# Attention projections in pairs of blocks: seven products of quarters for eight, score work in units of two tiles, smaller buffers

## The chip, the cores and the metric

The kernel runs on one core of one Trainium2 chip. The metric is device time in microseconds, the median of several executions. Engines: TensorE (PE), VectorE (DVE), ScalarE (ACT), GpSimd (POOL), SyncE (SP).

## The reference

One encoder layer on 1024 tokens of 1024 channels. The part that matters is the attention branch; the recurrent branch, the gates, the merge and a mixture of 16 experts follow it.

```python
h = _rmsnorm(x, norm_g)
proj = jnp.einsum('bsd,de->bse', h, w_in) + b_in
parts = jnp.split(proj, _split_points(), axis=-1)
...
for g, (window, dilation) in enumerate(ATTN_GROUPS):    # (128, 1), (512, 4), (2048, 16)
    shp = (B, S, HEADS_PER_GROUP, HEAD_DIM)             # 4 heads of 128
    q = _partial_rotary(q_parts[g].reshape(shp), cos, sin)
    k = _partial_rotary(k_parts[g].reshape(shp), cos, sin)
    v = v_parts[g].reshape(shp)
    o, lse = _dilated_window_attention(q, k, v, window // (2 * dilation), dilation)
    outs.append(o)
    lses.append(lse)
wts = jax.nn.softmax(jnp.stack(lses, axis=0), axis=0)
o = jnp.sum(wts[..., None] * jnp.stack(outs, axis=0), axis=0)
```

So for each of 4 heads and 3 groups there are three projections (q, k, v) of 1024 tokens from 1024 to 128 channels, 36 blocks of 128 channels in all.

## The kernel before

Stages follow one another: norm of x and its transposition, attention, recurrent branch and gates, merge and router, experts. Products are in float32 accuracy from reduced parts: each operand is split into a high and a low part (`split`: a cast on ACT for the high part, a subtraction on VectorE for the low), and `mm3` issues three matmuls (lines 51 to 53: high by high, high by low, low by high).

`norm_in` leaves the normed, transposed tokens in `hh` and `hl`, for each half h of the tokens [128, 8, 512]: 8 slices k of 128 channels by 512 tokens. `proj` loads no weights itself; it splits a [128, 8, 128] block `raw` into `wh`, `wl` and issues, for 2 halves by 8 slices, `mm3` into a PSUM tile `pj` of two banks: 48 matmuls of 128x512. The pool `pp` of `pj` has two such tiles and is opened ahead of `norm_in`.

`attn_head` runs a head's three groups and then combines them. `attn_group` makes q, k and v (`proj`, eviction with bias on ACT, line 260, or 243 and 245 for v with dilation under 16, which is laid out in slots of 64 keys; for q and k a rotation of the first 32 channels by a shuffle, two multiplications with the table `rot`, which stays in SBUF, and an addition, lines 264 to 268, on VectorE), transposes v (`pt`, then `vt`), and works through 8 tiles of 128 queries: scores into `ps` on TensorE, mask and row maximum on VectorE into `sc` and `stat` (line 293), minus the maxima (`nb`, line 295), exponentials with row sums on ACT, transposes into `pt`, copies to `pT` on VectorE (line 307), the products with `vt` into `po` (line 317), and copies into `og` on ACT (lines 320, 323). `og` is a ring of four buffers.

After the third group `stat` is transposed and copied to `stT` (line 333), stored to HBM and read back as `cs` in another layout; some small operations of ACT, VectorE and GpSimd (`wk`) turn it into three rows of weights, stored as `wg`. GpSimd then loads each row over all partitions into `wb` (one buffer), multiplies `og` by it, and sums into `ya`, which is stored (lines 365 to 371).

A scheduler at compile time sets the order in which each engine's instructions stand; each engine runs its own in that order. It mixes a group's TensorE work with the projections of the next blocks.

## Time and profile before

| what | us |
|---|---|
| median of 3 executions (2335.36 to 2339.7) | 2335.42 |
| the profiled execution's own time | 2332.01 |
| its span, first to last instruction | 2330.3 |
| TensorE busy in it | 2259.1 (97%) |
| VectorE busy | 1718.2 (74%) |
| ACT busy | 1391.7 (60%) |
| GpSimd busy | 217.4 (9%) |

The attention stage ends at about 537 us, the experts fill the second half. The rows for single stretches stand in the section of rows below; a row names the line of the kernel, the engine, the operation, and the tiles it writes and reads (out<-in).

### The profile page before, as it was taken

To read this page: it belongs to the slowest core of one execution; us is meant where nothing else is said; L and a number is where in the kernel's file an instruction comes from. 1 tells how busy PE (TensorE), PEld (TensorE's weight loads), DVE (VectorE), ACT (ScalarE), POOL (GpSimd) and SP (SyncE) were. 2 spreads that over 40 slices of the span, in tenths; PEclk is the share of its full clock that TensorE was granted. 3 is DMA by queue.
4 is the path that set the end of the run, shared out by engine and by line. 5 is a ranking of instruction groups with operands and counts; after the bars stand their busy time and mean duration, and the time that the engine had idled before them with its cause. 6 is when DMAs were issued, how large, how long until landed. Compare 5 with 4: busy or idle time off the path is not lost. (4 is left out here: it accounts for less than half of the span.)

```text
span 2330.3 us, 29850 instructions
## 1 busy us (share of the span) xinstructions
PE 2259.1 (97%) x10586; PEld 1852.4 (79%) x10586; DVE 1718.2 (74%) x2582; ACT 1391.7 (60%) x1725; POOL 217.4 (9%) x236
## 2 busy tenths in 40 slices
PE   7999999999999999999959999999999999999996
PEld 6887888887888888778847888888888888888884
DVE  7545454453455565678679999999999999999998
ACT  5332323324655666432137888888788888888886
POOL 1022030404000000100010000000000000000001
PEclk9999999999999999999979999999999999999999
DMA  4112121212322224745859999999999999999993
GB/s 151 37 37 80 31 82 37 74 37 87 104 77 81 69 68 150 240 159 168 320 190 338 381 380 378 377 389 389 388 379 380 380 377 389 395 385 380 378 388 127
DMA packets 238846, 539.20 MB, mean 231 GB/s; under 512 B 17628, under 2 KB 116376, under 8 KB 238696
## 3 DMA queue, kind: packets, MB, share of 16 engines
q1 hardware_dynamic: 224192, 488.70, 56.7%
q0 software_dynamic: 14400, 48.55, 6.3%
q8 instruction: 83, 1.36, 0.2%
q14 instruction: 67, 0.55, 0.1%
q10 hardware_dynamic: 104, 0.04, 0.0%
HBM read 501.35 MB, written 35.86 MB: 231 GB/s over the span
## 5 line engine op out<-in xcount | busy, mean ns | idle before, releaser
L46 DVE TENSOR_TENSOR elo<-et,ehi 128x1024 fp32r<-128x1024 f32 x549 | 648.2, 1223 | 76.3 <-ACT ehi L44 60.6
L44 ACT CAST ehi<-et 128x1024 fp32r<-128x1024 f32 x549 | 568.3, 1050 | 133.8 <-PE pg L53 89.4
L51 PE MATMUL pj<-hh,wh 128*128 128x512 f32 x1088 | 429.8, 395 | 2.1 <-ACT xp L389 2.0
L52 PE MATMUL pj<-hl,wh 128*128 128x512 f32 x1088 | 427.6, 393 | 0.0
L53 PE MATMUL pj<-hh,wl 128*128 128x512 f32 x1088 | 427.5, 393 | 0.0
L52 PE MATMUL pg<-elo,xgh 128*128 128x512 f32 x1032 | 407.6, 395 | 1.4 <-DVE elo L46 1.2
L51 PE MATMUL pg<-ehi,xgh 128*128 128x512 f32 x1032 | 403.6, 393 | 0.0
L53 PE MATMUL pg<-ehi,xgl 128*128 128x512 f32 x1032 | 402.8, 390 | 0.0
L44 ACT CAST wh<-raw 128x1024 fp32r<-128x1024 f32 (+1 forms) x100 | 98.2, 982 | 440.1 <-PE pj L52 267.8
L46 DVE TENSOR_TENSOR wl<-raw,wh 128x1024 fp32r<-128x1024 f32 x99 | 115.6, 1168 | 195.7 <-PE pj L53 191.1
L51 PEld LDWEIGHTS pj<-hh,wh 128*128 128x128 f32 x1088 | 204.7, 188 | 43.8 <-ACT xp L389 2.4
L53 PEld LDWEIGHTS pj<-hh,wl 128*128 128x128 f32 x1088 | 204.5, 188 | 41.2
L52 PEld LDWEIGHTS pj<-hl,wh 128*128 128x128 f32 x1088 | 204.8, 188 | 40.7
L52 PEld LDWEIGHTS pg<-elo,xgh 128*128 128x128 f32 x1032 | 194.2, 188 | 42.2 <-DVE elo L46 3.4
L51 PEld LDWEIGHTS pg<-ehi,xgh 128*128 128x128 f32 x1032 | 194.3, 188 | 41.1 <-ACT xgh L44 0.3
L53 PEld LDWEIGHTS pg<-ehi,xgl 128*128 128x128 f32 x1032 | 194.3, 188 | 39.4 <-DVE xgl L46 0.2
L52 PE MATMUL po<-elo,hdh 128*128 128x512 f32 x488 | 191.6, 393 | 4.0 <-DVE elo L46 4.0
L51 PE MATMUL po<-ehi,hdh 128*128 128x512 f32 x488 | 191.1, 392 | 1.7 <-ACT ehi L44 1.0
L53 PE MATMUL po<-ehi,hdl 128*128 128x512 f32 x488 | 190.0, 389 | 0.6 <-DVE hdl L46 0.6
L44 ACT CAST ehi<-raw 128x1024 fp32r<-128x1024 f32 x96 | 100.6, 1051 | 30.4 <-PE pg L53 21.7
L46 DVE TENSOR_TENSOR elo<-raw,ehi 128x1024 fp32r<-128x1024 f32 x96 | 114.5, 1221 | 3.3
L52 PEld LDWEIGHTS po<-elo,hdh 128*128 128x128 f32 x488 | 91.6, 188 | 25.5 <-DVE elo L46 6.1
(314 smaller groups left out, 3113.8 us busy)
## 6 DMA issues: line engine op xcount, KB each, us to landing
...
et<-w_down SPq DMA_DIRECT2D x177, 512.0 KB, 6.8
...
```

Of the source, the lines that this page charges most:

```text
L44: a = self.nc.scalar.copy(hi, src).ins
L46: b = (engine or self.nc.vector).tensor_sub(lo, src, f32(hi)).ins
L51: mm(ps, ah, bh, start=first, stop=False)
L52: mm(ps, ah, bl, start=False, stop=False)
L53: mm(ps, al, bh, start=False, stop=last)
```

## The change

The first two blocks (q and k of head 0, group 0) keep plain products (`one`), now in halves of 512 tokens. The other 34 are taken in pairs in the order of head, group, and q, k, v. For a pair with weights a and b, split by input channels into a1, a2 and b1, b2, and tokens split into quarters (`hq[c, h]`, 512 channels c by 512 tokens h), `pair` computes seven products of a 512x128 weight block by a quarter, 12 matmuls each, in place of eight. The combinations of the quarters, t1 to t4, are made once (`sums`), and those of the weights in each pair; two products are added to earlier ones in PSUM (`more`), the rest on VectorE when the result is put into place (`put`). t4 takes the place of the quarter b01, which is stored to HBM and loaded again behind the attention stage. Groups are called from `attention`, so that a group follows the pair that holds its v.

Beside this: PSUM tiles `pj` of one bank, four of them, in a pool opened behind `norm_in`; rotations in halves with `rot` loaded for each half, already in the group's order of tokens; scores, exponentials, transposes and products in units of two tiles (four for dilation 16), with `sc` and `pT` in two small buffers, `pT` copied on ACT, one `po` buffer; `og` in a ring of three, with the combined result formed in place in the first; `wb` in halves in one buffer, the small combination on 32 partitions.

```diff
-        self.hh = [self.hp.tile([128, 8, 512], FR, name=f"hh{h}") for h in range(2)]
-        self.hl = [self.hp.tile([128, 8, 512], FR, name=f"hl{h}") for h in range(2)]
+        self.hq = {(c, h): self.quarter(c, h) for h in range(2) for c in range(2)}
...
+    def weights(self, src, engine=None):
+
+        self.nw = (self.nw + 1) % 5
+        w = self.wp.tile([128, 2, 4, 128], FR, **({"name": "wh"} if self.nw < 3 else {"name": "wl", "bufs": 2}))
+        self.split(w[:, 0], w[:, 1], src, engine)
+        return w[:, 0], w[:, 1]
+
+    def times(self, ps, w, q, first, last, more=False):
+        for k in range(4):
+            self.mm3(ps, w[0][:, k], w[1][:, k], q[0][:, k], q[1][:, k], first and k == 0, last and k == 3, more)
+
+    def one(self, raw, out):
+
+        engine = self.nc.gpsimd if len(self.first_raws) == 2 else None
+        w = [self.weights(raw[:, 4 * c:4 * c + 4], engine) for c in range(2)]
+        for h in range(2):
+            ps = self.pp.tile([128, 512], F, name="pj")
+            for c in range(2):
+                self.times(ps, w[c], self.hq[c, h], c == 0, c == 1)
+            out(h, ps)
+
+    def sums(self, ap):
+
+        nc, hq = self.nc, self.hq
+        for part, q in enumerate(hq[0, 1]):
+            nc.sync.dma_start(self.s["b01"][part], f32(q).rearrange("p k t -> p (k t)"))
+        self.tq = [[self.tp.tile([128, 4, 512], FR, name=f"t{n}{part}") for part in "hl"] for n in range(3)]
+        rest = []
+        for c, name in enumerate(("vt", "qkv2")):
+            cs = slice(2 * c, 2 * c + 2)
+            t1, t2, t3 = [ap.tile([128, 2, 512], F, name="og", bufs=3) for _ in range(3)]
+            t4 = ap.tile([128, 2, 512], F, name=name)
+
+            def whole(t, *q):
+                hi, lo = [f32(a[:, cs]) for a in hq[q]]
+                nc.vector.tensor_add(t, hi, lo)
+
+            def parts(n, t):
+                self.split(self.tq[n][0][:, cs], self.tq[n][1][:, cs], t)
+
+            whole(t3, 0, 1)
+            whole(t1, 0, 0)
+            nc.vector.tensor_sub(t1, t3, t1)
+            whole(t2, 1, 1)
+            nc.vector.tensor_sub(t3, t2, t3)
+            nc.vector.tensor_sub(t2, t2, t1)
+            parts(1, t2)
+            parts(0, t1)
+            parts(2, t3)
+            whole(t4, 1, 0)
+            nc.vector.tensor_sub(t4, t4, t2)
+            rest.append((cs, t4))
+        q = self.quarter(0, 1)
+        for cs, t in rest:
+            self.split(q[0][:, cs], q[1][:, cs], t)
+        self.tq.append(q)
+
+    def pair(self, ap, a, b, outs):
+
+        nc, hq, (t1, t2, t3, t4) = self.nc, self.hq, self.tq
+        a1, a2, b1, b2 = a[:, :4], a[:, 4:], b[:, :4], b[:, 4:]
+        s = self.rp.tile([128, 2, 4, 128], F, name="raw128")
+        s1, s2 = s[:, 0], s[:, 1]
+        nc.vector.tensor_add(s1, b1, b2)
+        nc.vector.tensor_sub(s2, s1, a1)
+        p = lambda: self.pp.tile([128, 512], F, name="pj")
+        u, v = [ap.tile([128, 512], F, name="u" + n) for n in "12"]
+        pa = p()
+        self.times(pa, self.weights(a1), hq[0, 0], True, True)
+        nc.scalar.copy(u, pa)
+        pb = p()
+        self.times(pb, self.weights(s2), t2, True, True)
+        nc.vector.tensor_add(v, pb, u)
+        pc = p()
+        self.times(pc, self.weights(s1), t1, True, True)
+        nc.vector.tensor_sub(b1, a1, b1)
+        self.times(pb, self.weights(b1), t3, False, True, True)
+        nc.vector.tensor_add(u, pb, u)
+        outs[1](1, pc, u)
+        pd = p()
+        self.times(pd, self.weights(b2), t4, True, True)
+        outs[1](0, pd, u)
+        nc.vector.tensor_sub(s2, a2, s2)
+        self.times(pa, self.weights(a2), hq[1, 0], False, True, True)
+        outs[0](0, pa)
+        self.times(pc, self.weights(s2), hq[1, 1], False, True, True)
+        outs[0](1, pc, v)
+
...
+        n = S // d // 2
+        bias = self.b_in(j)
+        view = lambda a: a.rearrange("p (r l) -> p r l", r=d)
+
+        def out(half, ps, more=None):
+            if slots:
+                mid, end = view(t[:, :2 * d * (n - 64)]), view(t[:, 2 * d * (n - 64):])
+                to = [[(end[:, :, 64:], 0, 64), (mid[:, :, :n - 64], 64, n)],
+                      [(mid[:, :, n - 64:], 0, n - 64), (end[:, :, :64], n - 64, n)]][half]
+            else:
+                to = [(view(t)[:, :, half * n:half * n + n], 0, n)]
+            for o, a, b in to:
+                src = self.perm(ps, d)[:, :, a:b]
+                if more is None:
+                    nc.scalar.activation(o, src, AF.Identity, bias=bias)
+                else:
+                    nc.vector.scalar_tensor_tensor(o, src, bias, self.perm(more, d)[:, :, a:b], op0=OP.add, op1=OP.add)
+
+        return out
+
+    def rotate(self, ap, t, g):
+        nc = self.nc
+        for c in range(2):
+            cs = slice(c * 512, (c + 1) * 512)
+            rot = ap.tile([32, 2, 512], F, name="rot")
+            nc.sync.dma_start(rot, self.i["rot"][g, :, :, cs].rearrange("a p s -> p a s"))
+            sw = ap.tile([32, 512], F, name="sw")
+            x = t[0:32, cs]
+            nc.vector.stream_shuffle(sw, x, [(p + 16) % 32 for p in range(32)])
+            nc.vector.tensor_mul(sw, sw, rot[:, 1])
+            nc.vector.tensor_mul(x, x, rot[:, 0])
+            nc.vector.tensor_add(x, x, sw)
+
+    def attn_group(self, h, g, ap, stat, q, k, vT):
...
         tiles = self.tiles[g]
+        o = ap.tile([128, S], F, name="og", bufs=3)
...
+            sc = ap.tile([128, n, 512 // n], F, name="sc", bufs=2)
...
-            nc.vector.tensor_copy(pT[:, c:c + 4], p)
-
-        o = ap.tile([128, S], F, name="og", bufs=4)
...
+            nc.scalar.copy(pT, p)
+            if t0 % 4 == 0:
+                po = self.p3.tile([128, 4, 128], F, name="po")
...
-    def attn_head(self, h, ap):
+    def attention(self, ap):
+
+        blocks = [(h, g, w) for h in range(4) for g in range(3) for w in range(3)]
+        got = {}
+        og = []
+
+        def place(h, g, w):
+            t = got[h, g, w] = ap.tile([128, S], F, name=f"qkv{w}", bufs=2 if w == 0 else 1)
+            return self.put(t, DILS[g], 16 + 12 * w + 4 * g + h, w == 2 and DILS[g] < 16)
+
+        def finished(h, g, w):
+            if w < 2:
+                self.rotate(ap, got[h, g, w], g)
+                return
+            if g == 0:
+                self.stat = ap.tile([128, 3, 2, 8], F, name="stat", bufs=2)
+            og.append(self.attn_group(h, g, ap, self.stat, *[got.pop((h, g, i)) for i in range(3)]))
+            if g == 2:
+                self.combine(h, ap, self.stat, og)
+                og.clear()
+                if h == 0:
+                    self.decays(ap)
+
+        def load(b):
+            return self.first_raws.pop(0) if self.first_raws else self.load_w(*self.attn_cols(*b))
+
+        for b in blocks[:2]:
+            self.one(load(b), place(*b))
+        self.sums(ap)
+        for b in blocks[:2]:
+            finished(*b)
+        for n in range(2, len(blocks), 2):
+            two = blocks[n:n + 2]
+            raws = [load(b) for b in two]
+            self.pair(ap, *raws, [place(*b) for b in two])
+            for b in two:
+                finished(*b)
+
+    def combine(self, h, ap, stat, og):
         nc, s = self.nc, self.s
-        stat = ap.tile([128, 3, 2, 8], F, name="stat", bufs=2)
-        og = [self.attn_group(h, g, ap, stat) for g in range(3)]
...
-        y = ap.tile([128, S], F, name="ya", bufs=1)
+        nc.gpsimd.dma_start(s["wg"][h].rearrange("g (c i) -> c g i", c=C), wk[:, 0:3])
+        y = og[0]
         for g in range(3):
-            wb = ap.tile([128, S], F, name="wb", bufs=1)
-            src = s["wg"][h, g]
-            nc.gpsimd.dma_start(wb, bass.AP(tensor=src.tensor, offset=src.offset, ap=[[0, 128], [1, S]]))
-            if g == 0:
-                nc.gpsimd.tensor_mul(y, og[0], wb)
-            else:
-                nc.gpsimd.tensor_mul(wb, og[g], wb)
-                nc.gpsimd.tensor_add(y, y, wb)
+            for c in range(2):
+                half = slice(c * 512, (c + 1) * 512)
+                wb = ap.tile([128, 512], F, name="wb")
+                src = s["wg"][h, g, half]
+                nc.gpsimd.dma_start(wb, bass.AP(tensor=src.tensor, offset=src.offset, ap=[[0, 128], [1, 512]]))
+                nc.gpsimd.tensor_mul(og[g][:, half], og[g][:, half], wb)
+            if g:
+                nc.gpsimd.tensor_add(y, y, og[g])
         nc.gpsimd.dma_start(s["ya"][h], y)
 
 
@@ -451,21 +579,24 @@
...
-        self.pp = hs.enter_context(tc.tile_pool(name="pp", bufs=2, space=PSUM))
-        self.hp = hs.enter_context(tc.tile_pool(name="hp", bufs=1))
-        self.gp = self.hp
+        self.hp = hs.enter_context(self.pool("hp", 1))
+        self.nw = 4
         self.norm_in()
         with ExitStack() as c2:
             e2 = c2.enter_context
+            self.tp = e2(self.pool("tp", 1))
             ap = e2(self.pool("ap", 1))
+            self.pp = e2(self.pool("pp", 4, PSUM))
             self.p1 = e2(self.pool("p1", 1, PSUM))
             self.p2 = e2(self.pool("p2", 2, PSUM))
             self.p3 = e2(self.pool("p3", 1, PSUM))
...
-                self.attn_head(h, ap)
-                if h == 0:
-                    self.decays(ap)
+            self.attention(ap)
+        q = self.hq[0, 1] = self.quarter(0, 1)
+        for part in range(2):
+            nc.sync.dma_start(f32(q[part]).rearrange("p k t -> p (k t)"), self.s["b01"][part])
+        self.gp = hs.enter_context(self.pool("sg", 1))
+        self.pp = hs.enter_context(self.pool("pj", 2, PSUM))
```

Three places in the order of instructions. The first is TensorE at the start. `nps` are the norm's transposes, `pj` projections; before:

```order
L111 MATMUL nps<-ident,rows 128x16
L175 MATMUL nps<-ident,xt 128x128 x16
L51 MATMUL pj<-hh_81,wh 128x512
L175 MATMUL nps<-ident,xt 128x128 x4
L52 MATMUL pj<-hl_83,wh 128x512
L53 MATMUL pj<-hh_81,wl 128x512
L175 MATMUL nps<-ident,xt 128x128 x4
```

After (the products follow in the same manner):

```order
L111 MATMUL nps<-ident,rows 128x16
L174 MATMUL nps<-ident,xt 128x128 x32
L117 MATMUL nps<-ident,rows 128x124
L118 MATMUL nps<-ident,rows 128x48
L174 MATMUL nps<-ident,xt 128x128 x32
L51 MATMUL pj<-b00h,wh 128x512
```

The projection matmuls that stood between the transposes now stand behind all of them.

The second is VectorE of the changed kernel behind the plain blocks: t0 to t2 hold t1 to t3 of the code, `b01l_556` is the low part of t4, `wh_616` the weights of the second product (`pb`) of the first pair; line 359 to 362 are a rotation. Ahead of these rows stand 15 more of `sums`, and a shuffle.

```order
L46 TENSOR_TENSOR t0l_514<-og_537,t0h_513 128x1024
L252 TENSOR_TENSOR og_538<-og_538,og_537 128x1024
L46 TENSOR_TENSOR t2l_518<-og_539,t2h_517 128x1024
L257 TENSOR_TENSOR qkv2_540<-qkv2_540,og_538 128x1024
L46 TENSOR_TENSOR t1l_516<-og_538,t1h_515 128x1024
L46 TENSOR_TENSOR b01l_556<-vt_522,b01h_555 128x1024
L46 TENSOR_TENSOR b01l_556<-qkv2_540,b01h_555 128x1024
L360 TENSOR_TENSOR sw_563<-sw_563,rot_561 32x512
L361 TENSOR_TENSOR qkv0_393<-qkv0_393,rot_561 32x512
L46 TENSOR_TENSOR wh_616<-raw128_593,wh_616 128x512
L362 TENSOR_TENSOR qkv0_393<-qkv0_393,sw_563 32x512
L46 TENSOR_TENSOR wh_633<-raw128_593,wh_633 128x512
```

The split of `wh_616`, for which the second of its matmuls waits, stands behind all sums and in the middle of a rotation. Before, no such rows exist.

The third is the combination of head 0, where GpSimd's queue and ACT's meet. GpSimd before (`og_637`, `og_912`, `og_1171` are the outputs of the three groups of head 0):

```order
L360 DMA scr_wg<-wk_1196 8x3x128
L365 DMA wb_1214<-scr_wg 128x1024
L367 TENSOR_TENSOR ya_1213<-og_637,wb_1214 128x1024
L365 DMA wb_1217<-scr_wg 128x1024
L369 TENSOR_TENSOR wb_1217<-og_912,wb_1217 128x1024
L370 TENSOR_TENSOR ya_1213<-ya_1213,wb_1217 128x1024
L365 DMA wb_1221<-scr_wg 128x1024
```

GpSimd after (`og_732`, `og_992`, `og_1385` are those outputs):

```order
L488 DMA scr_wg<-wk_1455 32x3x32
L495 DMA wb_1472<-scr_wg 128x512
L496 TENSOR_TENSOR og_732<-og_732,wb_1472 128x512
L495 DMA wb_1475<-scr_wg 128x512
L496 TENSOR_TENSOR og_732<-og_732,wb_1475 128x512
L495 DMA wb_1478<-scr_wg 128x512
L496 TENSOR_TENSOR og_992<-og_992,wb_1478 128x512
L495 DMA wb_1481<-scr_wg 128x512
L384 MEMSET sc_1760 128x64
L496 TENSOR_TENSOR og_992<-og_992,wb_1481 128x512
L498 TENSOR_TENSOR og_732<-og_732,og_992 128x1024
```

ACT after, in the first group of head 1, whose output `og_1694` is copied from `po`:

```order
L399 COPY pT_1748<-pt_1749 128x512 [waits PE_49]
L411 COPY og_1694<-po_1713 128x512 [waits Pool_49]
L44 CAST wh_1895<-raw128_1788 128x512 [waits PE_49]
L399 COPY pT_1770<-pt_1771 128x512 [waits PE_49,Activation_49]
L411 COPY og_1694<-po_1755 128x512 [waits PE_49]
```

The first copy of `og_1694` waits for GpSimd: it has the buffer of `og_992`, which line 498 is the last to read. Ahead of that line GpSimd now has four loads, each behind the multiplication that frees `wb`, and a memset of `sc_1760`, the last unit of the same group of head 1.

## Rows read from the trace of the kernel before

**Rows 1.** The page's head, and of its slices (40 equal ones, busy share in tenths) those of TensorE and VectorE.

```profile
span 2330.3 us, 29850 instructions
...
PE   7999999999999999999959999999999999999996
...
DVE  7545454453455565678679999999999999999998
```

**Rows 2.** The busy time of each engine in stretches of the attention stage (length, busy us and instructions by engine, granted clock, DMA share, GB/s).

```profile
0.00:16.90 16.90, 4.71 (x17) 3.14 (x17) 8.79 (x34) 9.57 (x19) 6.05 (x14) 1.00 0.92 319
16.90:60.00 43.10, 43.06 (x203) 34.99 (x204) 34.87 (x90) 22.40 (x36) 1.80 (x6) 1.00 0.29 79
60.00:200.00 140.00, 137.69 (x706) 112.92 (x705) 70.53 (x122) 45.59 (x106) 25.09 (x31) 1.00 0.17 50
200.00:400.00 200.00, 198.96 (x982) 163.61 (x981) 102.00 (x154) 59.56 (x119) 29.47 (x36) 1.00 0.17 51
400.00:560.00 160.00, 157.07 (x784) 128.24 (x783) 73.92 (x128) 52.20 (x112) 39.13 (x53) 1.00 0.20 59
```

**Rows 3.** TensorE's groups by line and shape from 0 to 540 us: the first of the three projection matmuls (busy us, mean ns of one, idle before).

```profile
L51 PE MATMUL pj<-hh,wh 128*128 128x512 f32 x590 | 235.8, 400 | 0.1
```

**Rows 4.** TensorE's order of time within one projection (start us, us, instruction).

```profile
43.31 0.39 PE L52 MATMUL pj<-hl,wh 128*128 128x512 f32 x1
...
43.99 0.39 PE L52 MATMUL pj<-hl,wh 128*128 128x512 f32 x1
```

**Rows 5.** ACT's order of time: weight casts, each released by the end of the projection whose weights it overwrites (the first has one behind it in time), and the copy of a head's statistics, in heads 0 and 1.

```profile
47.18 1.05 ACT L44 CAST wh<-raw 128x1024 fp32r<-128x1024 f32 x1 [5.64 <-issue]
...
58.06 1.05 ACT L44 CAST wh<-raw 128x1024 fp32r<-128x1024 f32 x1 [8.81 <-issue]
...
156.03 0.30 ACT L333 COPY stT<-pt 48x128 f32<-48x128 f32 x1
...
283.71 0.29 ACT L333 COPY stT<-pt 48x128 f32<-48x128 f32 x1
```

**Rows 6.** TensorE's order of time at the start: the first projection matmuls, one at full pace, the last transposes of the norm.

```profile
16.94 0.80 PE L51 MATMUL pj<-hh,wh 128*128 128x512 f32 x1
...
18.49 0.78 PE L52 MATMUL pj<-hl,wh 128*128 128x512 f32 x1
...
23.27 0.40 PE L53 MATMUL pj<-hh,wl 128*128 128x512 f32 x1
...
34.45 0.60 PE L175 MATMUL nps<-ident,xt 128*128 128x128 f32 x4
```

**Rows 7.** VectorE's order of time at the start: a norm eviction series (five in one row), the last normalised tile, the series behind it.

```profile
16.92 3.43 DVE L178 SCALAR_TENSOR_TENSOR hl<-nps,cG,hh 128x512 fp32r<-128x512 f32 x5 [1.23 <-ACT hh L177]
...
29.12 0.75 DVE L171 TENSOR_SCALAR xt<-xt,rs_r 128x1024 f32<-128x1024 f32 x1
31.39 5.36 DVE L178 SCALAR_TENSOR_TENSOR hl<-nps,cG,hh 128x512 fp32r<-128x512 f32 x8 [1.52 <-ACT hh L177]
```

**Rows 8.** VectorE's groups by line and shape over the whole span: a split of 128x512, and a sum of 128x512 with one input in PSUM (`pq`).

```profile
L536 DVE TENSOR_TENSOR raw<-raw,pq 128x512 f32<-128x512 f32 x16 | 10.9, 682 | 19.1 <-PE pq L53 19.1
...
L46 DVE TENSOR_TENSOR rgl<-rgw,rgh 128x512 fp32r<-128x512 f32 x8 | 5.5, 692 | 11.3 <-ACT rgh L44 11.3
```

**Rows 9.** VectorE's groups by line and shape from 0 to 540 us: weight splits, the four operations of a rotation, the copies of transposed scores, and `nb`.

```profile
L46 DVE TENSOR_TENSOR wl<-raw,wh 128x1024 fp32r<-128x1024 f32 x37 | 45.7, 1236 | 129.7 <-PE pj L53 129.7
L266 DVE TENSOR_TENSOR sw<-sw,rot 32x1024 f32<-32x1024 f32 x24 | 41.1, 1711 | 0.8
L267 DVE TENSOR_TENSOR qkv<-qkv,rot 32x1024 f32<-32x1024 f32 x24 | 40.6, 1691 | 0.0
L264 DVE STREAM_SHUFFLE sw<-qkv 32x1024 f32<-32x1024 f32 x24 | 31.4, 1306 | 0.0
L268 DVE TENSOR_TENSOR qkv<-qkv,sw 32x1024 f32<-32x1024 f32 x24 | 29.5, 1230 | 0.8
L307 DVE COPY pT<-pt 128x512 f32<-128x512 f32 x40 | 27.7, 692 | 46.0 <-PE pt L306 46.0
...
L295 DVE TENSOR_SCALAR nb<-stat 128x8 f32<-128x8 f32 x12 | 3.8, 316 | 0.4
```

**Rows 10.** VectorE's order of time in head 1's first group: one `nb`.

```profile
190.12 1.90 DVE L295 TENSOR_SCALAR nb<-stat 128x8 f32<-128x8 f32 x1
```

**Rows 11.** GpSimd's order of time in the combination of head 0.

```profile
156.62 0.53 POOL L334 DMA_DIRECT2D scr_st<-stT  x1 [1.76 <-ACT stT L333]
...
175.81 0.61 POOL L365 DMA_DIRECT2D wb<-scr_wg  x1 [1.49 <-DMA scr_wg<-wk]
180.59 2.40 POOL L367 TENSOR_TENSOR ya<-og,wb 128x1024 f32<-128x1024 f32 x1 [4.17 <-DMA wb<-scr_wg]
183.29 0.59 POOL L365 DMA_DIRECT2D wb<-scr_wg  x1 [0.30 <-POOL ya L367]
187.16 2.37 POOL L369 TENSOR_TENSOR wb<-og,wb 128x1024 f32<-128x1024 f32 x1 [3.29 <-DMA wb<-scr_wg]
189.61 2.37 POOL L370 TENSOR_TENSOR ya<-ya,wb 128x1024 f32<-128x1024 f32 x1
```

**Rows 12.** Stretches of the router, where TensorE has little to do (columns as in group 2; the clock is the number behind the engines).

```profile
1180.00:1190.00 10.00, 0.38 (x1) 0.09 (x1) 8.92 (x71) 1.44 (x3) 3.08 (x3) 0.50 0.65 263
...
1200.00:1210.00 10.00, 3.33 (x12) 2.76 (x13) 5.06 (x6) 1.17 (x2) 3.52 (x2) 0.50 0.79 266
```

137 lines of the change are left out of this document (52 added, 85 removed).

## The prediction

> **What bounds the kernel now.** The page says it first: TensorE is busy in almost every fortieth of the span, VectorE in about half of the slices up to the ninth [rows 1]. The attention stage lies in the first 540 us; cut into stretches, from 60 us on TensorE is busy 137.7 of 140, 199.0 of 200 and 157.1 of 160 us, VectorE 70.5, 102.0 and 73.9, ACT about a third [rows 2]. So there the time is TensorE's count of matmuls, and whatever makes it wait is new. A modelled matmul duration is not its price: the group says 396 to 400 ns [rows 3], but three starts are 0.68 us apart, 0.2267 us each [rows 4]. Two weight casts, each released by the end of a projection, are 10.88 us apart, which is 48 x 0.2267 [rows 5]. ACT's copies of two heads' statistics (`stT`) lie 127.7 us apart [rows 5]: nine projections (97.9) and three groups of scores and outputs, about 9.9 us each.
>
> The diff ends with the attention stage: behind it both programs issue the same rows in the same order, with one 2 MB reload between. What is won or lost up to 540 us shifts the rest.
>
> **Products removed.** 17 pairs of blocks take 7 x 12 = 84 matmuls, not 96: 204 x 0.2267 = 46.2 us, 2.72 us a pair. 16 of these pairs count in full, -43.5 us; the first is in the next sum. The two additions inside PSUM (pa, pb, pc used again) cost nothing on TensorE.
>
> **The start.** Before, projections fill the gaps between the norm's transposes: the first `pj` matmul stands at 16.9 us, the last transpose at 34.5 [rows 6]. The second projection ends at 47.2, the third at 58.1 [rows 5], so four (without a group) end near 69.0. After, the pool `pp` opens behind the pool of the transposes, and all 64 transposes precede the first product. VectorE gets, ahead of the last normalised tile (29.1 us, before the evictions at 31.4 [rows 7]), two 128x1024 additions and six ops of 128x512, less one 128x1024 split: 2 x 1.2 + 6 x 0.68 - 1.2 = 5.3 us, so the last transposes end near 40.5. The two plain blocks (96 x 0.2267 = 21.8) end near 62.5, `pa` at 65.2. `pb` needs the low part of its weights, and on VectorE this split stands behind 22 ops of 128x1024, which follow the last eviction (36.8 + 5.3 = 42.1): 22 x 1.2 = 26.4, and four small ones, 2.5, so about 71 (69.5 to 73). The other 72 matmuls take 16.3, and further splits hold them up 0 to 3 us: the pair ends at 86 to 90 against 69.0. I take **+19.5 us** (17 to 23). The gate bears on the upper end: at 16.9 to 19 us matmuls took 0.8 us, from 23 us on 0.4 [rows 6]; a burst behind a sparse stretch starts slow.
>
> **VectorE's new work.** By kinds: 119 splits of 128x512 at 0.69 [rows 8] for 34 of 128x1024 at 1.24 [rows 9], +40 us; 68 sums of weight quarters, 46; 34 sums with PSUM, 23 (L536 reads PSUM: 0.682 [rows 8]); 51 half evictions, which ACT did, near 0.75 (L178 reads PSUM: 3.43/5 to 0.75 [rows 7]), 38 to 55 as strided ones are unpriced; the sums, 27. Off: 40 `pT` copies, -27.7, which go to ACT. Rotations: 24 x (1.71 + 1.69 + 1.31 + 1.23) = 143 [rows 9] become 192 halves at about 0.65, some 125, since the strided table reads go. In all about +130: half busy becomes nearly four fifths.
>
> A queue that full no longer hides. Three places per pair wait for it: the second use of `pb` (its first eviction), the second use of `pc`, and, with a group behind the pair, the transposes of v, which wait for the last eviction behind two rotations. Where a pair is (q, k), eight rotation halves (5.2 us) and the pair's seven splits, four sums and five evictions (11.3) fall into 19.0 us of products with VectorE idle for the pair's last 2 to 3 us: just late. I walked such pairs through order and rows: five (v, q) pairs come 0.7 to 3.7 us late, 7.5 in all; scores and evictions inside the twelve groups 0.5 each, 6; the end 2. In this kernel VectorE is also held by GpSimd: `nb` took 1.90 us where its mean is 0.316 [rows 9, 10], while GpSimd's 2.37 us addition of 189.61 ran [rows 11]. Each head has some 12 us of such work, now beside a fuller VectorE; 2 us for all four. Together **+17 us** (5 to 45).
> The Trainium skill ("SBUF — State Buffer", section "Who interferes with whom") says that a VectorE instruction with two SBUF inputs contends with a GpSimd instruction that reads SBUF, and the one that issues first locks the other out. The row of `nb` agrees in that the lock lasts to the other's end, though `nb` has one SBUF input. By the rule every added split or sum that meets one of these multiplications would wait out the rest of it; that would be an estimated 10 us more than the 2 taken, and 2362 in place of the sum below.
>
> **One og buffer fewer.** The rings give the next head's g0 output the buffer of this head's g1 output, free when y += g1 is done. Before, a fourth was free. GpSimd's chain runs from the store of the statistics (156.62) over the first `wb` issue (175.81) to y += g1, which ends at 191.98 [rows 11], 36 us after the copy at 156.03 [rows 5]. After, four half loads are in series, each waiting for the multiplication that frees the single buffer. A whole load took 4.8 and 3.9 us from issue to use, a multiplication 2.4 [rows 11]; a half should be 3.3 to 4.3 and 1.25, with 0.3 to reissue, 5.2 in the middle. So 19 + 4 x 5.2 + 2.4 = 42 us (38 to 44; the 32-row chain before it may be 1 to 2 shorter). The next head's g0 copy comes after 1.3 pairs (25 us) in heads 1 and 3 (counted from 0), where k and v make the next pair, and after 2 (38) in head 2. ACT waits in that copy, with a cast and the next `pT` copy behind it; `po` has one buffer, so TensorE waits. The `sc` memset of the same unit stands in GpSimd's queue behind three of these multiplications, and a transpose waits for it. Less the lateness of TensorE itself, 12 us twice: **+24 us** (2 x 5 to 2 x 17). Head 2 costs about nothing. Where TensorE stood still in the router its clock was 0.50 for more than 20 us [rows 12]; here full work follows at once, so 0 to 4 more, inside the range.
>
> **Costed at nothing**, with the cover: the store of b01 (2 MB) and the 48 rotation loads on SP meet a DMA share of 0.17 to 0.29 [rows 2]; its reload takes 6.6 us at the 319 GB/s of the start [rows 2] and has 12 us of other products ahead of its use (in the open it would be 6.6 us, once); a rotation load is issued when the half before it has been multiplied, and a late one would hold VectorE by its 2 us or so, counted in the 5 to 45; ACT gets the 40 copies for the 51 half evictions.
>
> **Sum.** -43.5 + 19.5 + 17 + 24 = +17.0 us. The profiled execution has 2332.01 us (span 2330.3), 3.4 below the median of 2335.42; on the median the sum gives 2352.
>
> **The rivals.**
> *The saving comes through* (faster): VectorE's lateness falls where TensorE has group work to put in between, 4 us, and half loads take 2 us, so that y += g1 is done at 30 and costs 2 x 2. -43.5 + 19.5 + 4 + 4 = -16: 2319; with a start of 17 and no og wait 2313. For it: TensorE's rows of groups and of the next pair are finely mixed. Against: the row of `wb` loads, and one `po`. It decides when og waits and VectorE's lateness together are under 24 us.
> *Short og waits, the rest as forecast*: 2 x 4, -43.5 + 19.5 + 17 + 8 = +1: 2336.
> *VectorE becomes the bound*: each pair ends 2.7 us late, the saving gone: -43.5 + 19.5 + 45 + 20 = +41: 2376. For it: strided PSUM evictions are unpriced, and GpSimd's lock. Against: 75 to 80% is not 100.
>
> **Chances.** Forecast (2341 to 2366) 0.45, saving through 0.22, short og waits 0.18, VectorE bound 0.15. The middle case straddles the line: a measurement of this kernel tells about 0.2%, 4.7 us, from no change. Faster 0.25, same 0.14, slower 0.61. The range for 8 in 10 runs from within the first rival to the last: 2319 to 2377; the forecast's own is 2341 to 2366.
>
> **What the profile will show.** Right: the first `pj` matmul near 40 us; a TensorE gap of 4 to 8 us near 65 to 71 that ends with VectorE's `wh` split; two gaps of 8 to 16 us whose releaser is ACT's og copy (or GpSimd's memset), near the first products of heads 1 and 3; VectorE 75 to 80% busy from 90 to 540 us; attention's last `po` near 554, not 537. Wrong: half loads of `wb` under 2.5 us, strided evictions above 1.1 us, or transposes that mix with products after all.

## The result and the profile after

| | before | after |
|---|---|---|
| median, us | 2335.39 (4 executions, 2333.07 to 2339.7) | 2363.66 (4, 2362.0 to 2366.15) |
| ratio | | 1.0131, 95% interval 1.0118 to 1.0143 |
| profiled execution (its span), us | 2332.01 (2330.3) | 2364.6 (2362.6) |
| TensorE busy in it, us | 2259.1 | 2233.2 |
| VectorE busy | 1718.2 | 1842.7 |

The changed kernel is slower by 28 us (1.2%) by the two medians; the ratio on record is 1.0131, which is 31 us. The profiled executions differ by 32.6. The prediction was 2352 us, in 2319 to 2377, with 0.61 for slower: the side was right and the range held, the size was 11 us short by the medians. TensorE lost 26 us of busy time, less than the 46.2 us of matmuls left out; a part of the difference is slow-clock time, which the modelled durations carry in them.

The page of the changed kernel, the slices of TensorE and VectorE, against [rows 1]:

```profile
PE   6998979899999999999959999999999999999996
...
DVE  8985876764444656569578999999999999999998
```

VectorE is fuller in the first quarter, and TensorE shows eights and a seven there where it had nines. Two stretches of its attention stage, to be held against [rows 2] (columns as there):

```profile
200.00:300.00 100.00, 90.01 (x456) 73.45 (x455) 67.85 (x148) 39.45 (x94) 15.61 (x22) 0.97 0.21 64
300.00:400.00 100.00, 86.34 (x422) 70.79 (x421) 67.69 (x138) 35.97 (x81) 27.21 (x43) 0.93 0.21 64
```

TensorE is busy 90.0 and 86.3 of 100 us, where it was 199.0 of 200. The clock is 0.97 and 0.93, where the row before had 1.00. VectorE is busy 68% in these two, and 322.0 of 450 us (72%) from 90 to 540 us, not the 75 to 80% that I had reckoned.

TensorE's groups with waits from 90 us to the end of the stage (line, tiles, count; busy us, mean ns; idle before them, by what ended it):

```profile
L405 PE MATMUL po<-pT,vt 128*128 128x128 f32 x320 | 48.3, 298 | 14.7 <-ACT og L411 13.3 <-ACT pT L399 1.3
...
L398 PE MATMUL pt<-ident,sc 128*128 128x128 f32 x160 | 31.3, 282 | 15.8 <-POOL sc L384 13.2 <-ACT sc L394 2.0 <-issue 0.4
...
L388 PE MATMUL ps<-qkv,qkv 128*128 128x192 f32 x78 | 17.5, 335 | 0.8 <-DVE qkv L362 0.6 <-DVE stat L389 0.2
...
L371 PE MATMUL pt<-ident,qkv 128*128 128x128 f32 x88 | 14.2, 283 | 5.3 <-DVE qkv L347 4.5 <-ACT vt L372 0.5
...
L388 PE MATMUL ps<-qkv,qkv 128*128 128x128 f32 x64 | 11.9, 283 | 2.2 <-DVE qkv L362 2.1
...
L51 PE MATMUL pj<-b11h,wl 128*128 128x512 f32 x24 | 10.1, 422 | 1.9 <-DVE qkv L347 1.9
```

Waits that end with the og copy or the `sc` memset sum to 13.3 + 13.2 = 26.5 us, waits that end with VectorE to 0.8 + 4.5 + 2.1 + 1.9 = 9.3. The one wait for an exponential, 2.0 us, is a late `nb` of VectorE, which GpSimd held (below, in the part on the prediction); the expectations count it with og, as 28.5 in all. In order of time the start and the largest of them (in brackets the idle time before the instruction, and what ended it):

```profile
39.73 0.80 PE L51 MATMUL pj<-b00h,wh 128*128 128x512 f32 x1 [0.71 <-DVE b11l L178]
...
68.97 0.50 PE L53 MATMUL pj<-t1h,wh 128*128 128x512 f32 x1 [0.32 <-DVE wh L46]
...
83.80 0.49 PE L371 MATMUL pt<-ident,qkv 128*128 128x128 f32 x3
...
207.83 0.33 PE L398 MATMUL pt<-ident,sc 128*128 128x128 f32 x1 [1.24 <-POOL sc L384]
...
214.85 2.07 PE L405 MATMUL po<-pT,vt 128*128 128x128 f32 x8 [6.69 <-ACT og L411]
...
354.87 0.47 PE L398 MATMUL pt<-ident,sc 128*128 128x128 f32 x1 [9.05 <-POOL sc L384]
...
466.79 0.33 PE L398 MATMUL pt<-ident,sc 128*128 128x128 f32 x1 [2.95 <-POOL sc L384]
...
473.74 2.08 PE L405 MATMUL po<-pT,vt 128*128 128x128 f32 x8 [6.61 <-ACT og L411]
```

GpSimd in the combination of head 0, which answers to [rows 11], and ACT's copy of the statistics that starts it (first row):

```profile
176.62 0.31 ACT L461 COPY wk<-pt 48x128 f32<-48x128 f32 x1
```

```profile
190.46 0.63 POOL L495 DMA_DIRECT2D wb<-scr_wg  x1 [1.43 <-DMA scr_wg<-wk]
...
194.23 1.28 POOL L496 TENSOR_TENSOR og<-og,wb 128x512 f32<-128x512 f32 x1 [3.13 <-DMA wb<-scr_wg]
...
195.81 0.59 POOL L495 DMA_DIRECT2D wb<-scr_wg  x1 [0.30 <-POOL og L496]
...
200.08 1.28 POOL L496 TENSOR_TENSOR og<-og,wb 128x512 f32<-128x512 f32 x1 [3.68 <-DMA wb<-scr_wg]
...
207.60 0.18 POOL L384 MEMSET sc<- 128x64 f32 x1
...
211.85 2.33 POOL L498 TENSOR_TENSOR og<-og 128x1024 f32<-128x1024 f32 x1
```

From the copy (176.62) to the end of y += g1 (214.18) it takes 37.6 us. The first two half loads take 3.8 and 4.3 us from issue to use where a whole one took 4.8 and 3.9 [rows 11]: half the bytes bought little. From the first issue on it is 23.7 us, as forecast (4 x 5.2 + 2.4); the small combination ahead of it took 13.8 where I had 19. The `sc` memset stands at 207.60, and TensorE's transpose of 207.83 follows it at once; the products of 214.85 follow the og copy.

Last, behind the attention stage: two instructions that stand in the same place in both kernels, the first matmul of the recurrent stage that waits for `xp`, and the first of the merge that waits for `sgt`. Before:

```profile
554.71 0.50 PE L51 MATMUL pj<-hh,wh 128*128 128x512 f32 x1 [1.97 <-ACT xp L389]
...
930.54 0.50 PE L51 MATMUL pq<-et,wh 128*128 128x512 f32 x1 [1.31 <-ACT sgt L381]
```

After:

```profile
572.05 0.50 PE L51 MATMUL pj<-b00h,wh 128*128 128x512 f32 x1 [1.92 <-ACT xp L517]
...
958.29 0.50 PE L51 MATMUL pq<-et,wh 128*128 128x512 f32 x1 [4.10 <-ACT sgt L509]
```

The distance is 17.3 and 27.8 us, and 32.3 at the end of the span. So about half of the loss lies in the attention stage, and half behind it, where the two programs issue the same rows.

### The profile page after: what moved, and what is told of

It reads as the page before. It is cut to its first block, busy times and chain, and to the rows that moved or that the text cites. A ratio compares the mean times of both kernels' runs of the same rounds, so it can differ in the third digit from the quotient of the medians.

```text
span 2362.6 us, 30231 instructions
## 1 busy us (share of the span) xinstructions
PE 2233.2 (95%) x10382; PEld 1826.5 (77%) x10382; DVE 1842.7 (78%) x2965; ACT 1437.7 (61%) x1850; POOL 211.7 (9%) x284
## 4 chain that ended last, share of the span: by engine, by line
PE 75%; DVE 9%; DMA 8%; POOL 3%; issue 3%; ACT 2%; POOLq 0%; SPq 0%; ACTq 0%; DVEq 0%
PE pg L52 10%; PE pg L51 10%; PE pg L53 10%; PE pj L53 6%; PE pj L51 6%; PE pj L52 6%; PE po L52 5%; PE po L53 5%; PE po L51 5%; DMA wb<-scr_wg 3%; PE pq L51 2%; PE pq L53 2%; PE pq L52 2%; PE po L405 2%; POOL og L496 1%
## 5 line engine op out<-in xcount | busy, mean ns | idle before, releaser
L44 ACT CAST wh<-raw 128x512 fp32r<-128x512 f32 (+1 forms) x139 | 106.6, 769 | 255.9 <-PE pj L53 77.9
L46 DVE TENSOR_TENSOR wl<-raw,wh 128x1024 fp32r<-128x1024 f32 (+1 forms) x64 | 69.5, 1085 | 68.2 <-PE pj L53 57.3
L51 PEld LDWEIGHTS po<-ehi,hdh 128*128 128x128 f32 x488 | 91.6, 188 | 21.4 <-ACT ehi L44 1.4
L53 PEld LDWEIGHTS po<-ehi,hdl 128*128 128x128 f32 x488 | 91.7, 188 | 19.8 <-DVE hdl L46 1.1
L1009 POOL DMA_INDIRECT scr_x<-eo,idx x15 | 23.8, 1585 | 890.8 <-ACT eo L1008 890.8
L46 DVE TENSOR_TENSOR elo<-wh,ehi 128x1024 fp32r<-128x1024 f32 x72 | 85.2, 1220 | 11.9 <-ACT ehi L44 9.5
L44 ACT CAST ehi<-wh 128x1024 fp32r<-128x1024 f32 x72 | 73.9, 1050 | 15.0 <-PE pg L53 11.9
L51 PE MATMUL pq<-et,wh 128*128 128x512 f32 x192 | 75.6, 394 | 4.1 <-ACT sgt L509 4.1
```

What stands on the lines that cost most here:

```text
L44: a = self.nc.scalar.copy(hi, src).ins
L46: b = (engine or self.nc.vector).tensor_sub(lo, src, f32(hi)).ins
L51: mm(ps, ah, bh, start=first, stop=False)
L53: mm(ps, al, bh, start=False, stop=last)
L1009: nc.gpsimd.indirect_dma_start(out=s["x1"], out_offset=bass.IndirectOffsetOnAxis(ap=idx[:, :1], axis=0), in_=eo, in_offset=None, compute_o ...
```

## The experiments

Each run's ratio is to executions of the kernel before on the same chip (median 2333.2, 2333.8 and 2333.0 us in the three groups of four runs); differences to the changed kernel are taken from ratios times 2335.4. Of each kernel there is one trace, so a difference of a few us between two rows of different runs carries the spread of single executions: those of one kernel lie 2 to 12 us apart here.

### The loads behind the og wait

```diff
-                wb = ap.tile([128, 512], F, name="wb")
-                src = s["wg"][h, g, half]
-                nc.gpsimd.dma_start(wb, bass.AP(...))
+                wb = f32(self.hq[1, c][0][:, g])
                 nc.gpsimd.tensor_mul(og[g][:, half], og[g][:, half], wb)
```

> The changed kernel with the loads of wb left out: GpSimd multiplies og by a tile that already lies in SBUF (the weights of the combination are not applied), with the same number of multiplications and additions. Theory A (the series of half loads holds og and the sc memset, TensorE waits, its clock falls, and the late store of the combined head holds the recurrent stage): the waits of 7.9, 11.0 and 9.6 us at the three head boundaries fall to under 2 us in all, some 8 us of slow clock behind them and some 6 us at the start of the recurrent stage go too: 2322 us, 2316 to 2330. Rival B (VectorE is late by as much, and these waits only cover it): VectorE's waits grow by what goes, 2345 to 2356.

Measured: 2334.55 us, ratio 1.0007 (0.9995 to 1.0018), 29 us less than the changed kernel; between the two theories, nearer A. No wait at a head boundary is left that names og or a memset, but VectorE's grew there:

```profile
184.44 0.79 PE L51 MATMUL pj<-t2h,wh 128*128 128x512 f32 x1 [4.49 <-DVE u L279]
...
313.19 0.76 PE L51 MATMUL pj<-t2h,wh 128*128 128x512 f32 x1 [3.18 <-DVE u L279]
...
438.36 1.69 PE L388 MATMUL ps<-qkv,qkv 128*128 128x192 f32 x4 [2.73 <-DVE qkv L362]
```

These three, 10.4 us in all, were covered before: while TensorE stood waiting for og, VectorE had caught up. The `xp` row stands at 549.93, 22.1 us earlier than in the changed kernel: so the og waits of 26.5 us, and the slow clock behind them, were worth less than their length. The wait for the stored head at the start of the recurrent stage was gone (below), which is most of the rest of the 29.

The same with nothing left out, by two buffers:

```diff
-            pT = ap.tile([128, 4, 128], F, name="pT", bufs=2)
+            pT = ap.tile([128, 4, 128], F, name="pT")
-                wb = ap.tile([128, 512], F, name="wb")
+                wb = ap.tile([128, 512], F, name="wb", bufs=2)
```

> The changed kernel with two wb buffers, so that two half loads are under way, and the memory for it from pT, which has one buffer and no longer two. Theory A: y += g1 ends some 28 us behind the statistics' copy in place of 37.6, the og waits nearly vanish (25 of 28.5 us), with 7 us of clock and 6 us of the recurrent stage, less 0 to 8 us for pT: 2328 us, 2320 to 2340. Rival B (a load's time is its share of one queue, so two take twice as long): 2358 to 2366.

Measured: 2334.41 us, ratio 1.0012 (0.9999 to 1.0026): 28 us less, as with no loads at all. The loads overlap, which refutes B:

```profile
189.66 1.19 POOL L495 DMA_DIRECT2D wb<-scr_wg  x2 [1.43 <-DMA scr_wg<-wk]
...
203.47 2.35 POOL L498 TENSOR_TENSOR og<-og 128x1024 f32<-128x1024 f32 x1
```

Two issues stand in the first row, and y += g1 ends 16 us behind them, not 24 as above. It came out inside A. What A had hoped for beyond 28 us stands against waits for VectorE (4.92 us ahead of the transposes at 324.48) and for `pT` (3.14 us at 207.47).

### The memset

```diff
-                        nc.gpsimd.memset(sc[:, t - t0, z:z + 64], 0.0)
+                        nc.vector.memset(sc[:, t - t0, z:z + 64], 0.0)
```

> The changed kernel with the sc memsets on VectorE in place of GpSimd, nothing else. Theory A: the memset is a wait of its own where og would have been free by then, between heads 1 and 2: its 9.0 us go, with some 2 us of slow clock; at the other two boundaries the og copy ends at the same time as before and takes over the memset's 1.2 and 2.9 us: 2352 us, 2348 to 2357. Rival B: the og copy takes the place of the memset at all three boundaries: 2361 to 2365.

Measured: 2355.02 us, ratio 1.0093 (1.0063 to 1.0122), 9 us less (the intervals of the two kernels overlap a little; all four executions lie below B): A. Between heads 1 and 2 nothing of the 9.05 us came back; at the other two the og copy took over the memset's part (8.28 for 7.93, and at the last more than that, 12.86 for 9.56):

```profile
213.67 2.08 PE L405 MATMUL po<-pT,vt 128*128 128x128 f32 x8 [8.28 <-ACT og L411]
...
466.84 2.07 PE L405 MATMUL po<-pT,vt 128*128 128x128 f32 x8 [12.86 <-ACT og L411]
```

### Plain products in the changed frame

```diff
-        for b in blocks[:2]:
-            self.one(load(b), place(*b))
-        self.sums(ap)
...
-            self.pair(ap, *raws, [place(*b) for b in two])
+            for b in two:
+                self.one(load(b), place(*b))
```

The reload of b01 behind the stage goes with it.

> The changed kernel with plain products for all 36 blocks (no sums, no pairs of seven), everything else as changed: buffers, rings, halves, units of two tiles, the pool order. Theory A (the buffers cost more than the seven products save): against the kernel before, 12 us at the start (all transposes ahead of the first product, and a low clock), some 20 us of og and memset waits, 5 us of clock, 7 us at the start of the recurrent stage: 2378 us, 2368 to 2388, so slower than the changed kernel. Rival B (the cost lies in VectorE's sums and evictions): 2335 to 2350.

Measured: 2413.99 us, ratio 1.035 (1.0325 to 1.0376): slower than the changed kernel by 51 us, on A's side and far beyond it. The frame alone costs 80 us. One part of that is an artefact: without the sums' memory the first tiles of the recurrent stage lie on the last head's og. By the profiled executions (`xp` row at 600.37) 28 us of the difference to the changed kernel arise in the attention stage and 24 behind it.

```profile
634.88 1.28 ACT L501 ACT_TABLE_LOAD   x1 [34.56 <-DMA scr_ya<-og]
```

```profile
641.50 0.79 PE L51 MATMUL pg<-xch,rgh 128*128 128x512 f32 x1 [28.33 <-ACT xch L44]
```

ACT waits 34.56 us for the store of the combined head, TensorE 28.33 behind it. That is the mechanism of the changed kernel's own loss behind the attention stage, grown large. There ACT's row is this one, and two waits of TensorE, of 2.23 us at 625.32 and 2.39 us at 638.93, stand behind it:

```profile
616.72 1.06 ACT L552 ACTIVATE sq<-a 128x1024 f32<-128x1024 f32 x1 [9.86 <-DMA scr_ya<-og]
```

With the loads gone or doubled no instruction of the stage waits for that store. Their `xp` matmuls (no loads, then two buffers):

```profile
549.93 0.50 PE L51 MATMUL pj<-b00h,wh 128*128 128x512 f32 x1 [3.36 <-ACT xp L515]
```

```profile
548.83 0.50 PE L51 MATMUL pj<-b00h,wh 128*128 128x512 f32 x1 [1.92 <-ACT xp L517]
```

From there to the span's end (2332.0 and 2331.5) it takes 1782.1 us (no loads) and 1782.7 (two buffers), against 1790.6 in the changed kernel and 1775.6 before. So about 8 of the 15 us behind the attention stage are the late store. The other traces agree but for one: 1789.2 to 1793.0 us where ACT waited over 9 us for that store (memset_dve, early_pp, early_four), 1778.7 to 1780.7 where no row waits for it (best1, best2, best1_plain, best1_gp); best1_norot took 1787.2 without such a wait. The other 7 us stayed with the late store gone. In the run with two buffers they arise in the merge (925 to 1050 us): 3.3 in TensorE's wait for `sgt` at its start, 4.59 us where it was 1.31, and the rest within 90 us behind it; best1_plain below has only 3 of the 7. ACT's `sgt` stands there behind weight casts, of which one waited 3.10 us for its load where it waited 1.30 before. What delays these loads was not found.

### The start

```diff
+            self.pp = e2(self.pool("pp", 4, PSUM))
+            self.norm_in()
             self.tp = e2(self.pool("tp", 1))
             ap = e2(self.pool("ap", 1))
-            self.pp = e2(self.pool("pp", 4, PSUM))
```

> The changed kernel with the pool of the projections' PSUM tiles opened ahead of the norm, so that the products of the two plain blocks stand between the transposes again. Theory A (the start is set by VectorE's sums: the first product pair needs them whatever TensorE did until then): the plain blocks end near 48 us, TensorE then waits some 15 us, and the low part of the second product's weights comes 1 to 4 us sooner than at 68.9; a clock drop may follow the wait: 2360 us, 2356 to 2364. Rival B (it is set by the transposes standing ahead of the products): 14 us less, 2347 to 2352.

Measured: 2376.23 us, ratio 1.0185 (1.0165 to 1.0204): 13 us more. B is refuted; A's wait came as forecast, with a price that A had not given it:

```profile
70.76 0.79 PE L51 MATMUL pj<-t1h,wh 128*128 128x512 f32 x1 [15.26 <-ACT wh L44]
```

```profile
69.33 0.67 DVE L271 TENSOR_TENSOR raw<-raw,raw 128x512 f32<-128x512 f32 x1
```

```profile
70.00:75.00 5.00, 4.24 (x10) 3.29 (x11) 5.00 (x11) 1.27 (x3) 0.00 (x0) 0.50 0.07 26
```

TensorE stands 15.26 us, to 70.76, where the changed kernel waited to 68.97: the cast that it waits for needs VectorE's weight sum of 69.33, which stands behind `sums`. The clock falls meanwhile and is 0.50 when the products begin. The first pair ends at 91.94, not 83.80, so 8 of the 13 us arise here; the rest come between there and the `xp` row, and were not followed. Filled with two more plain blocks (t4's second half in the tiles u1 and u2):

```diff
-        for b in blocks[:2]:
+        for b in blocks[:4]:
             self.one(load(b), place(*b))
         self.sums(ap)
...
-        for n in range(2, len(blocks), 2):
+        for n in range(4, len(blocks), 2):
```

> As the run before, but with the first four blocks plain and 16 pairs of seven products, so that TensorE has 21.8 us more of plain products while VectorE makes the sums. Theory A: the four blocks end near 69 us as in the kernel before, the sums are ready by then or 1 to 3 us later; against the changed kernel, whose fourth block ends at 83.8 us, some 12 us less: 2352 us, 2347 to 2356. Rival B (the sums come late by what the plain blocks' splits put ahead of them): under 6 us less, 2358 to 2363.

Measured: 2360.58 us, ratio 1.0112 (1.0094 to 1.013), 4 us less: B's range, though not B's cause, since TensorE waits nowhere for the sums. The start gained 7 of A's 12 us: the four blocks end at 76.79, where A had 69 and the changed kernel 83.80, and a wait that stood at 187.67 there stands at 180.24. At the next boundary the gain was partly given back:

```profile
207.00 2.08 PE L412 MATMUL po<-pT,vt 128*128 128x128 f32 x8 [8.63 <-ACT pT L406]
...
351.47 0.47 PE L405 MATMUL pt<-ident,sc 128*128 128x128 f32 x1 [10.15 <-POOL sc L391]
```

8.63 and 10.15 us where 1.24 + 6.69 and 9.05 stood, and longer waits for VectorE between. The `xp` wait of the recurrent stage stands at 569.80, so 2.3 of 7.4 us are left there. The 4 us are close to the noise: the two intervals overlap.

### Together

The edits of early_four, wb_two and memset_dve in one kernel:

```diff
+            self.pp = e2(self.pool("pp", 4, PSUM))
+            self.norm_in()
...
+        for b in blocks[:4]:
...
+                        nc.vector.memset(sc[:, t - t0, z:z + 64], 0.0)
...
+            pT = ap.tile([128, 4, 128], F, name="pT")
...
+                wb = ap.tile([128, 512], F, name="wb", bufs=2)
```

> The changed kernel with the early pool and four plain blocks, two wb buffers (pT in one), and the sc memsets on VectorE. The two wb buffers alone gave 29 us against the changed kernel; the start adds some 12 by theory A, the memsets little now that GpSimd's queue is short: 2321 us, 2315 to 2327, under the kernel before by 0.4 to 0.8%. Rival B (VectorE's lateness takes up what the other waits leave): 2328 to 2334, no difference from the kernel before.

Measured: 2327.05 us, ratio 0.9972 (0.9962 to 0.9981): faster than the kernel before by 6.5 us, at the edge between A and B.

The same with the memsets back on GpSimd:

```diff
-                        nc.vector.memset(sc[:, t - t0, z:z + 64], 0.0)
+                        nc.gpsimd.memset(sc[:, t - t0, z:z + 64], 0.0)
```

> Early pool, four plain blocks and two wb buffers as in best1, but the sc memsets on GpSimd as in the changed kernel. Theory A (the memset only costs where GpSimd's queue is held by loads): with the short queue it costs nothing and VectorE has 40 small operations less: 2326 us, 2322 to 2330. Rival B (it still waits behind multiplications at each head): 2331 to 2336.

Measured: 2330.42 us, ratio 0.9986 (0.9975 to 0.9998). Its interval overlaps that of best1, and it lies between the two theories: undecided.

best1 with plain products (the edit of plain_all, and the memory of the sums set aside):

```diff
+            pad = [[self.tp.tile([128, 4, 512], FR, name=f"t{n}{part}") for part in "hl"] for n in range(3)]
+            for t in sum(pad, []):
+                nc.gpsimd.memset(f32(t[0:1, 0, 0:1]), 0.0)
```

> best1 with plain products for all 36 blocks, no sums, and as much memory set aside (one element written in each tile) as the sums held, so that the tiles of the later stages lie where they lay. Theory A (with the og wait gone, the seven products bring their saved matmuls less VectorE's lateness): TensorE has 40 us more to do, no waits for VectorE and no sums: 2344 us, 2338 to 2350. Rival B (VectorE's lateness and the sums eat the whole saving): 2325 to 2333.

Measured: 2351.22 us, ratio 1.0084 (1.0067 to 1.0101). Just above A: in this frame 16 pairs of seven products save 26 us of the 43.5 us of their matmuls. The frame itself costs 20 against the kernel before. The comparison also leaves out the store and reload of b01, which go with the sums.

### VectorE's share

Seven of eight operations of each rotation left out, first in the changed kernel, then in best1:

```diff
-            nc.vector.stream_shuffle(sw, x, [(p + 16) % 32 for p in range(32)])
-            nc.vector.tensor_mul(sw, sw, rot[:, 1])
-            nc.vector.tensor_mul(x, x, rot[:, 0])
-            nc.vector.tensor_add(x, x, sw)
+            if c == 0:
+                nc.vector.tensor_mul(x, x, rot[:, 0])
```

> The changed kernel with seven of the eight VectorE operations of each rotation left out (q and k are not rotated), some 110 us of VectorE's work in the attention stage; the table loads stay. Theory A (TensorE waits for VectorE about 10 us in all, the rest of VectorE's work is hidden): these 10 us go, but TensorE reaches the og waits earlier and stands there 2 to 4 us longer: 2356 us, 2350 to 2360. Rival B (VectorE is close to the bound of the stage, its lateness runs on from pair to pair): below 2346.

> best1 with seven of the eight VectorE operations of each rotation left out (q and k are not rotated). Theory A (what is left between best1 and the 43.5 us of the removed products is mostly VectorE's lateness): its waits of some 14 us go, with their clock drops: 2313 us, 2309 to 2318. Rival B (it is elsewhere): 2322 to 2327.

Measured: 2355.14 us, ratio 1.0095 (1.0078 to 1.0112), 8.5 us less in the first. That is A's number, but only a part of it came A's way: the `xp` row (569.23) stands only 2.8 us earlier than in the changed kernel: waits for VectorE fell by 5 us and those for og and the memset grew from 26.5 to 30.7. In the profiled execution the other 7.2 us lie behind the stage, where the late store held less:

```profile
606.95 1.06 ACT L550 ACTIVATE sq<-a 128x1024 f32<-128x1024 f32 x1 [4.51 <-DMA scr_ya<-og]
```

ACT waits 4.51 us there, not 9.86, and no wait of TensorE stands behind it. A had not named this, so its number is partly luck. In the second run 2330.25 us, ratio 0.9985 (0.9975 to 0.9995): not faster than best1, so A fell; B's 2322 to 2327 was too low too. Its `xp` row stands 3.8 us ahead of best1's (543.49 against 547.32), and the rest took 6.5 us longer, for which no cause was found. TensorE's waits up to that row are as long as in best1, 24.8 against 23.3 us, but now 19.9 of them are for `pT` (3.6 in best1) and 4.7 for VectorE (15.6). The largest:

```profile
200.01 2.08 PE L410 MATMUL po<-pT,vt 128*128 128x128 f32 x8 [8.76 <-ACT pT L404]
```

```profile
198.88 0.58 ACT L416 COPY og<-po 128x512 f32<-128x512 f32 x1 [8.79 <-POOL og L503]
```

TensorE waits for `pT`, and the `pT` copy stands behind the og copy, which waits for GpSimd's y += g1. Another of 8.89 us stands at 443.88. In best1 itself the longest waits near these two places were 1.86 us (for an exponential) and 3.15 us (for `pT`). The lateness of VectorE and the wait for og lie side by side; who takes away one finds the other.

Two of four weight sums on GpSimd:

```diff
-        nc.vector.tensor_add(s1, b1, b2)
-        nc.vector.tensor_sub(s2, s1, a1)
+        nc.gpsimd.tensor_add(s1, b1, b2)
+        nc.gpsimd.tensor_sub(s2, s1, a1)
```

> best1 with two of the four weight sums of each pair (s1 and the first s2) on GpSimd in place of VectorE, 32 operations of 128x512 by 0.67 us off VectorE, some 1.25 us each on GpSimd. Theory A (VectorE's relief counts, GpSimd has room): 4 us less, 2323 us, 2319 to 2326. Rival B (GpSimd's operations hold VectorE's two-input operations, or stand behind the wb loads): 2328 to 2338.

Measured: 2359.17 us, ratio 1.0118 (1.0101 to 1.0135), 34 us more than best1: B, and more. VectorE now waits for GpSimd and TensorE for VectorE:

```profile
L289 DVE TENSOR_TENSOR raw<-raw,raw 128x512 f32<-128x512 f32 x16 | 15.3, 954 | 28.5 <-POOL raw L277 28.5
```

TensorE's longest waits for VectorE are 7.23 us at 341.92 and 6.94 at 468.51. VectorE sat idle 28.5 us ahead of L289 until GpSimd's sum ended, and L289 itself took 954 ns on average where best1 has 712. Both halves of B are there, the queue and the held operand; this run doesn't part them.

## Why the prediction was right or wrong

The stage up to the recurrent products came out at +17.3 us, as the sum said (+17.0). The agreement is in part luck: of the terms one was right, and those that were off cancel:

| term | predicted | in the profile after |
|---|---|---|
| products, 16 pairs | -43.5 | -43.5 (pace unchanged) |
| start, to the end of the first pair | +19.5 | +14.8 (83.80 against 69.0) |
| VectorE's lateness | +17 (5 to 45) | +11.3 in waits (9.3, and 2.0 with GpSimd's hold) |
| og wait | +24 | +26.5 (17.5 at the two places priced, 9.05 at the third) |
| slow clock behind waits | 0 to 4, not in the sum | about +7.5 |
| sum | +17.0 | +16.6 (17.3 between the two `xp` rows) |

**The start.** The transposes ended where I had them (first product 39.73, forecast 40.5), and the low clock cost the first ten matmuls 2 us (the eleventh starts at 44.17; 44.17 - 39.73, less 2.27). The wait for the second product's weights was 0.32 us, not 4 to 8: the split came at 68.9 (forecast 71), and in the order TensorE has eight matmuls that need no low part ahead of it, six of them of later products. early_pp shows that VectorE's sums set this place: with the plain blocks done earlier TensorE only waited for them.

**VectorE.** Half again too high, inside its bounds. The added work was sized right, 124.5 us against "about +130". The share was not: 225.9 us of 450 before, and with 130 less the 27 of the sums, which lie ahead of 90 us, some 329 of 467 us, which is 70% and not nearly four fifths. The evictions, of which the strided forms had no price before, took 1.0 us in the mean of 37, near the upper bound:

```profile
L347 DVE SCALAR_TENSOR_TENSOR qkv<-pj,cA,u 128x512 f32<-128x512 f32 x37 | 37.5, 1016 | 9.5 <-PE pj L53 9.5
```

Yet the lateness is partly hidden where TensorE waits for og anyhow: no_wb_loads uncovered 10 us of it. The terms are not a sum but partly the longer of two; the prediction added them.

GpSimd's hold on VectorE, 2 us in the sum, shows in one wait of TensorE. VectorE, GpSimd, ACT and TensorE in turn:

```profile
339.04 2.30 DVE L391 TENSOR_SCALAR nb<-stat 128x2 f32<-128x2 f32 x1
```

```profile
338.66 2.67 POOL L498 TENSOR_TENSOR og<-og 128x1024 f32<-128x1024 f32 x1
```

```profile
341.44 0.51 ACT L394 ACTIVATE sc<-sc,nb 128x256 f32<-128x256 f32 x1 [2.51 <-DVE nb L391]
```

```profile
342.09 0.93 PE L398 MATMUL pt<-ident,sc 128*128 128x128 f32 x4 [1.96 <-ACT sc L394]
```

This `nb` ends with GpSimd's addition (341.34 and 341.33), where others of its kind take 0.15 us. From 90 to 560 us nine VectorE instructions that met a multiplication or addition of GpSimd took an estimated 10.7 us more in all than the median of their kind. How much of that stands in TensorE's other 9.3 us of waits for VectorE was not parted. The rule of the Trainium skill ("SBUF — State Buffer", section "Who interferes with whom"), that a VectorE instruction with two inputs in SBUF contends with a GpSimd instruction that reads SBUF, agrees in kind: six of the nine have two such inputs, and took 0.56 to 2.1 us longer, and in best1_gp, with GpSimd busier, L289 went from 712 to 954 ns. The 10 us more that the prediction worked out by that rule came about on VectorE; of TensorE's waits only these 1.96 us can be told apart as theirs.

**The og wait.** Place and releaser were right: two waits of 7.9 and 9.6 us where 12 each were forecast, inside the bounds, from a chain of 37.6 us (forecast 38 to 44). Wrong was "head 2 costs about nothing": 9.05 us there are the `sc` memset (354.64), which stands in GpSimd's queue behind the last two loads, the second sum and the store's issue, although og was free from 341.33. The prediction had named it as an accompaniment, not as a wait of its own; memset_dve gave 9 us back. That the term as a whole came out near 24 is luck.

**The clock.** The step "full work follows at once, so 0 to 4 more" was undersized. TensorE is busy without a gap behind five of its waits, at half clock:

```profile
187.70:190.70 3.00, 3.00 (x7) 2.37 (x8) 3.00 (x7) 0.00 (x0) 1.27 (x5) 0.50 0.03 4
214.90:217.70 2.80, 2.80 (x12) 2.70 (x13) 0.69 (x1) 0.90 (x2) 0.21 (x4) 0.50 0.44 120
331.00:334.00 3.00, 3.00 (x11) 2.54 (x11) 3.00 (x8) 1.19 (x4) 1.89 (x2) 0.51 0.16 55
354.90:357.80 2.90, 2.90 (x10) 2.52 (x11) 0.00 (x0) 0.59 (x1) 0.32 (x3) 0.50 0.46 186
473.80:477.20 3.40, 3.40 (x15) 3.30 (x16) 0.69 (x1) 0.89 (x2) 0.69 (x4) 0.50 0.57 141
```

15.1 us at 0.50 are 7.5 us of work lost. One of the five follows a wait of 1.92 us (187.67), one a wait of 2.23 us (329.91).

**Behind the stage.** The step that failed is the one the prediction didn't price: "What is won or lost up to 540 us shifts the rest." The combination of the last head is part of that chain too, and it ends after the attention stage: the recurrent stage's tiles lie on the combined og, and ACT waited 9.86 us for its store. The late store cost about 8 us, and the merge 7 more that remain unexplained. Of these 15 us the medians show 11, by which the forecast was short; the profiled pair lies 4 us further apart than the medians.

**The rivals.** "The saving comes through" had the right condition: without the og waits the kernel stands at the time of before (wb_two 1.0012). "VectorE becomes the bound" did not come true: best1 without rotations is no faster, though its TensorE waits only changed their cause. That the seven products themselves don't pay is not borne out: they give 26 us in best1's frame; in the changed one 51, about half of it behind the stage, with the artefact above. Of the signs, the gap at 65 to 71 us and VectorE's 75 to 80% did not come, and the last `po` ended at 559.1, not 554: 5 us of this are gone again at the `xp` row, with 19 matmuls fewer between the two than before (51 against 70). None of the signs of being wrong came.
